# Two-layer hybrid block on one core: variances placed earlier, squares of the second half later, evenly dealt pieces, reordered first loads and last residuals

## The chip, the cores and the metric

The kernel runs on one core of one Trainium2 chip. The metric is the device time of one execution in microseconds. A core has TensorE (PE, matrix products into PSUM), VectorE (DVE), ScalarE (ACT), GpSimd (POOL) and SyncE (SP, whose queue issues most DMAs).

## The reference

All numbers are fp32; one sequence of 512 tokens, width 1024, two layers. What is computed:

```
for layer in range(2):
    a = rmsnorm(h, ln_mix_pre[layer]);  mem_n = rmsnorm(mem, ln_mem[layer])    # mem: 256 x 1024
    if layer == 0:
        u, v, q_mem = split(a @ w_in_a)                    # 768, 768, 256
        main = chunked_spatial_gating(u, v, ...)
    else:
        kvf = rmsnorm(h, ln_shared) @ w_shared_kv          # keys 768, values 768, 12 forget gates
        q, q_mem = split(a @ w_in_b)
        main = forgetting_attention(q, k, v, log_sigmoid(gates + b_forget))    # 12 heads of 64, causal
    mixed = concat(main, memory_attention(q_mem, mem_n, w_mem_kv[layer]))      # 4 memory heads
    h = h + rmsnorm(mixed @ w_out[layer], ln_mix_post[layer])
    f = rmsnorm(h, ln_ffn_pre[layer])
    f = (silu(f @ w_gate) * (f @ w_up)) @ w_down           # 1024 -> 2816 -> 1024
    h = h + rmsnorm(f, ln_ffn_post[layer])
```

The forgetting attention adds c_i - c_j to the logits, where c is the running sum of the log gates over the tokens. The last h is the output.

## The kernel before

**Products.** Each fp32 operand is split into a high part (a cast on ScalarE) and a low part (a subtraction on VectorE), and a product is three matmuls of such parts, lines 193 to 195: hi by hi, hi by lo, lo by hi. Weights come by DMA into tiles named raw; `split` makes whi and wlo of them (L241), `scaled_parts` (L245, L246) does the same with a gain. Most matmuls have 512 or 256 columns.

**Layout.** h holds the residual stream with the 1024 features as 8 blocks of 128 partitions and the 512 tokens along the row. The root mean square of a token is thus a sum over partitions: squares are added up on VectorE (acc, L279; for pairs of blocks sq, L320 and L322), multiplied by a column of 1/1024 on TensorE (st, L290), eps is added on VectorE (var, L292), GpSimd takes the power -1/2 (r, L262), TensorE spreads the result over the partitions (rb, L259), and VectorE copies it to rbc or rmem (L305) or uses it from PSUM. `Norm.finish` is the part up to r, `Norm.spread` the rest. Where tokens lie on partitions (the end of a mixer or an FFN, and value blocks) the scale is a column and is applied by ScalarE.

**Order.** The program is written as one stream of calls, and a list scheduler turns it into one list of instructions per engine. It takes them by the place in the program, `tc.high_priority()` moves what is inside it ahead, and `tc.issue_after(x)` (also through `behind`) holds an instruction until x stands. Engines run their lists in order and wait on semaphores.

**Start (layer A).** `layer_a` loads two blocks of query weights (raws, 128 x 1024 each) and the tokens. Per block k of the features TensorE multiplies both weight blocks with `ahi`, `alo`; behind the first products stand idle matmuls on zeros. Then come three value blocks in pieces (a piece is four blocks k for 128 tokens, 12 matmuls of 256 columns), among which the token norm, the memory's sums (`mem_sums`), its scaled inputs (`mem_inputs`, tiles mparts) and its key weights stand. `mem_project` makes the memory's keys and values.

**Boundary.** `boundary` joins the end of a mixer (or of an FFN) to the next projection. `tail(tb)` finishes 128 tokens and leaves them as y with tokens on partitions; `turn(half, pairs)` transposes y back (yt, L821), adds it to h (`residual`, L826), makes the scaled input of the next product and its squares (`nnorm.pair`). A `group` runs four weight blocks over the first half of the tokens; the turns of the second half hang in it after steps k = 3 and 5, and the norm of the first half after 6. Before the FFNs `combined` then adds and subtracts quarters of the inputs (lines 931 to 936), as a fast matrix product needs.

**Heads of layer B.** `attend` runs 4 memory heads and 12 forgetting heads one after the other, each in fixed steps (logits S, softmax N, transposes T, values V). At its F steps it takes pieces out of `between[n]`: for n = 0 to 11 those of the key and value projections (48 pieces: value block 0, key blocks 0 and 1, value block 1, key blocks 2 and 3 and so on), for n = 12 to 16 those of the output projection. `forget` makes the log gates (ScalarE and VectorE), `cumulate` their running sums (cs, 8 matmuls, L1251; then cc, four copies and differences, L1255 to L1258), and `head_parts` copies rows of cc and of the split queries and keys into qa, qc, ka, kc by DMAs of SP (L1281 to L1284).

**End.** `give(tb, ...)` transposes the FFN's result of 128 tokens back, adds it to h and stores it; for the last tokens this is four groups of two blocks, whose stores alternate between the queues of SP and ScalarE.

Of the kernel before, what the change touches and what calls it, by code (L numbers as in the profile page):

```python
# [40 lines left out]
def hybrid(ctx: ExitStack, tc: tile.TileContext, i: dict, out: bass.AP):  # L41
# [222 lines left out]
    class Norm:  # L264
# [16 lines left out]
        def finish(self, cols):  # L281

            c0, c1 = cols
            tbs = range(c0 // P, c1 // P)
            t0, t1 = c0 // P, c1 // P
            st = ps("tr", (P, 4), s="st")
            for tb in tbs:
                some = self.sums(tb, cols)
                for n, sq in enumerate(some):
                    PE.matmul(st[:, tb : tb + 1], sq, avg, start=n == 0, stop=n == len(some) - 1)  # L290
            v = small("var")
            V.tensor_scalar_add(v[:, t0:t1], st[:, t0:t1], RMS_EPS)  # L292
            rsqrt(self.r4[:, t0:t1], v[:, t0:t1], t1 - t0)

# [270 lines left out]
    def layer_a():  # L565
# [18 lines left out]
        tokens(0, 1)  # L584
        query_weights(1, 0, 1024)
        tokens(1, 2)
        tokens(2, 4)
        query_weights(0, 512, 1024)
        tokens(4, 6)
        tokens(6, 8)  # L590
# [30 lines left out]
        with tc.tile_pool(name="sgu", bufs=1) as lp:  # L621
# [8 lines left out]
            def pieces(n):  # L630
                for f in take(fill, n):
                    f()
# [9 lines left out]
            pieces(1)  # L642
            pre.spread(FULL, rbc)
            qf = [plain("q") for _ in range(2)]
# [3 lines left out]
            pieces(1)  # L648
            xs = mem_inputs(0, memt)
            wk = mem_key_weights(0)  # L650
            norm.finish((0, NMEM))
            pieces(3)
            norm.spread((0, NMEM), rmem)
# [105 lines left out]
    def tail_of(xs, load, ys, eps=None, last=False):  # L759
# [7 lines left out]
        def urgent(tb):  # L767
            return tc.high_priority() if tb == TB - 1 and not last else ExitStack()

# [87 lines left out]
    def boundary(phase, post, pre, nnorm, dst, block, evac, scaled=None):  # L857
# [8 lines left out]

        def turn(half, pairs):
            cols = HALVES[half]
            c0, c1 = cols
            for j in pairs:  # L870
# [7 lines left out]
                if scaled is not None:  # L878
# [4 lines left out]
                    xs[j, half] = pair_parts("xs", scaled[j, half])  # L883
                nnorm.pair(j, cols)

        def inputs(half):
# [3 lines left out]
            return [tuple(t[:, c0:c1] for t in xs[k]) for k in range(KT)]  # L890

        tail(0)
        phase_parts = tuple(last_parts)
        tail(1)
        with behind(phase_parts):
# [6 lines left out]
        outs = group(ws, inputs(0), h0, ["mm", "lg"] * 2, lag=3,  # L902
                     after={3: lambda: turn(1, range(2)), 5: lambda: turn(1, range(2, 4)),
                            6: lambda: nnorm.finish(h0)})
        nnorm.spread(h0, dst)
        evac(outs, h0)
        outs = group(ws[:2], inputs(1), h0, ["mm", "lg"])
        nnorm.finish(h1)
# [5 lines left out]

        return xs, close

# [125 lines left out]
    def feed_forward(layer, phase, xp, meanwhile=None):  # L1042
# [39 lines left out]

        scaled = {}
        a, close = boundary(phase, G_MIX_POST + layer, G_FFN_PRE + layer, nnorm, rb, first, evac_first, scaled)
        w = [down_weights(layer, 0, dh) for dh in range(2)]
        close()
        xs, last = combined(a, scaled, xp)
        last()
# [40 lines left out]
    def layer_b(phase, fp):  # L1129
# [16 lines left out]
        def evac_first(outs, cols):  # L1146
            for m, o in zip(first, outs):
                queries(m, o, cols)

        a, close = boundary(phase, G_FFN_POST, G_MIX_PRE + 1, bnorm, rbc,  # L1150
                            lambda n: prepared(i["w_b_q"][first[n]], (KT, P)), evac_first)
# [150 lines left out]
        more = queue(outs)  # L1302
        between = {n: take(fill, c) for n, c in enumerate((5, 5, 5, 5, 4, 4, 4, 4, 3, 3, 3, 3))}
        between[1].insert(4, forget)
        between[2].insert(3, cumulate)
        for n, c in zip(range(12, 17), (2, 3, 3, 4, 4)):
# [19 lines left out]
    with tc.tile_pool(name="ffn1", bufs=4) as xp:  # L1326
        tail, ys = feed_forward(1, phase, xp)

    def give(tb, order, queues=(nc.sync,)):

# [15 lines left out]
    idle(8, zero, end)  # L1346
    give(TB - 1, (range(4, 6), range(2), range(6, 8), range(2, 4)), (nc.sync, nc.scalar))

# [60 lines left out]
```

## Time and profile before

| | |
|---|---|
| median of 3 runs | 1121.24 us (1120.61 to 1121.42) |
| the profiled execution | 1121.42 us |
| its span, first to last instruction | 1119.7 us |
| granted TensorE clock, mean | 0.999 |
| TensorE, VectorE, ScalarE, GpSimd busy | 1107.3, 892.0, 660.3, 28.5 us |
| instructions | 19536 |
| DMA traffic | 118.12 MB |

Busy times are sums over instructions; matmuls overlap in TensorE's pipeline, so that a busy TensorE can still pause. In a row of the timeline stand the start in us, the duration in us, the engine, the line of the kernel, the operation, the tiles (written <- read), the shapes and the count; brackets give the idle time of the engine just before it and what ended that.

### The profile page before, as it was taken

What the parts mean: (1) busy time and instruction counts of PE and PEld (TensorE: products, weight loads), DVE (VectorE), ACT (ScalarE), POOL (GpSimd) and SP (SyncE); (2) the same over time, 40 slices, a digit from 0 to 9 for tenths busy, and PEclk for the clock granted to TensorE, in tenths of its full rate; (3) what the DMA queues carried; (4) which work ended last, traced back from release to release, by engine and by line L of the source; (5) the groups of instructions that cost most, each with busy time, mean ns of one, the idle gap of its engine ahead of it and who ended that gap; (6) DMA issues with size and microseconds to landing.
All of it is one profiled execution on the core that took longest, in us unless ns stands there. A gap on an engine that the chain in (4) does not pass through costs nothing.

```text
span 1119.7 us, 19536 instructions
## 1 busy us (share of the span) xinstructions
PE 1107.3 (99%) x7409; PEld 1002.7 (90%) x7409; DVE 892.0 (80%) x1721; ACT 660.3 (59%) x1388; POOL 28.5 (3%) x41
## 2 busy tenths in 40 slices
PE   8999999999999999999999999999999999999998
PEld 6998889999899899998988898889999899899996
DVE  7979448999598578796968889958998598588776
ACT  7775458755266255476757677768765266255453
POOL 0100001000000000001000000001000000000000
PEclk9999999999999999999999999999999999999999
DMA  7413231334224234244242655421235234233222
GB/s 265 151 49 109 77 97 58 100 108 151 76 89 140 74 99 127 76 135 148 63 128 59 153 128 137 135 76 57 65 106 152 74 101 133 70 109 118 76 76 76
DMA packets 63557, 118.12 MB, mean 105 GB/s; under 512 B 5164, under 2 KB 39992, under 8 KB 63464
## 3 DMA queue, kind: packets, MB, share of 16 engines
q1 hardware_dynamic: 62584, 116.05, 33.8%
q8 instruction: 58, 0.95, 0.4%
q0 software_dynamic: 192, 0.52, 0.2%
q10 hardware_dynamic: 688, 0.31, 0.1%
q14 instruction: 35, 0.29, 0.1%
HBM read 104.71 MB, written 2.10 MB: 95 GB/s over the span
## 4 chain that ended last, share of the span: by engine, by line
PE 86%; DVE 7%; ACT 3%; issue 2%; POOL 1%; DMA 1%; SPq 0%; POOLq 0%; DVEq 0%; ACTq 0%
PE y L193 9%; PE y L195 9%; PE y L194 9%; PE a L194 5%; PE a L193 5%; PE a L195 5%; PE ps L195 3%; PE ps L194 3%; PE ps L193 3%; PE e L193 3%; PE e L194 3%; PE x L194 3%; PE x L193 3%; PE x L195 3%; PE e L195 3%; DVE wlo L241 2%
## 5 line engine op out<-in xcount | busy, mean ns | idle before, releaser
L241 ACT CAST whi<-raw 128x512 fp32r<-128x512 f32 x460 | 276.2, 620 | 267.0 <-PE y L195 118.6
L241 DVE TENSOR_TENSOR wlo<-raw,whi 128x512 fp32r<-128x512 f32 x460 | 305.2, 685 | 108.8 <-ACT whi L241 106.6
L193 PE MATMUL y<-whi,fhi 128*128 128x512 f32 (+1 forms) x356 | 140.0, 394 | 0.0
L194 PE MATMUL y<-wlo,fhi 128*128 128x512 f32 (+1 forms) x356 | 139.4, 392 | 0.0
L195 PE MATMUL y<-whi,flo 128*128 128x512 f32 (+1 forms) x356 | 139.4, 392 | 0.0
L194 PE MATMUL a<-xslo,whi 128*128 128x256 f32 x320 | 90.0, 281 | 0.0
L194 PE MATMUL x<-xslo,whi 128*128 128x256 f32 x320 | 89.9, 281 | 0.0
L195 PE MATMUL x<-xshi,wlo 128*128 128x256 f32 x320 | 89.9, 281 | 0.0
L193 PE MATMUL x<-xshi,whi 128*128 128x256 f32 x320 | 89.8, 281 | 0.0
L193 PE MATMUL a<-xshi,whi 128*128 128x256 f32 x320 | 89.8, 281 | 0.0
L195 PE MATMUL a<-xshi,wlo 128*128 128x256 f32 x320 | 89.8, 281 | 0.0
L193 PEld LDWEIGHTS y<-whi,fhi 128*128 128x128 f32 x356 | 66.9, 188 | 15.7 <-ACT fhi L241 0.7
L195 PEld LDWEIGHTS y<-whi,flo 128*128 128x128 f32 x356 | 66.9, 188 | 15.5 <-DVE flo L241 0.2
L194 PEld LDWEIGHTS y<-wlo,fhi 128*128 128x128 f32 x356 | 67.0, 188 | 14.7 <-DVE wlo L241 0.2
L193 PE MATMUL ps<-xshi,whi 128*128 128x256 f32 (+1 forms) x224 | 67.5, 304 | 0.0
L195 PE MATMUL ps<-xshi,wlo 128*128 128x256 f32 (+1 forms) x224 | 67.1, 302 | 0.1
L194 PE MATMUL ps<-xslo,whi 128*128 128x256 f32 (+1 forms) x224 | 66.4, 299 | 0.0
L193 PEld LDWEIGHTS a<-xshi,whi 128*128 128x128 f32 x320 | 60.4, 189 | 0.4
L194 PEld LDWEIGHTS a<-xslo,whi 128*128 128x128 f32 x320 | 60.3, 188 | 0.3
L193 PEld LDWEIGHTS x<-xshi,whi 128*128 128x128 f32 x320 | 60.4, 189 | 0.0
L195 PEld LDWEIGHTS x<-xshi,wlo 128*128 128x128 f32 x320 | 60.3, 189 | 0.0
L194 PEld LDWEIGHTS x<-xslo,whi 128*128 128x128 f32 x320 | 60.3, 188 | 0.0
(283 smaller groups left out, 3091.1 us busy)
## 6 DMA issues: line engine op xcount, KB each, us to landing
raw<-in_w_gate SPq DMA_DIRECT2D x44, 512.0 KB, 3.6
raw<-in_w_up SPq DMA_DIRECT2D x44, 512.0 KB, 3.5
raw<-in_w_down SPq DMA_DIRECT2D x44, 512.0 KB, 4.0
raw<-in_w_out SPq DMA_DIRECT2D x16, 512.0 KB, 4.5
raw<-in_w_b_q SPq DMA_DIRECT2D x8, 512.0 KB, 3.5
raw<-in_w_a_v SPq DMA_DIRECT2D x6, 512.0 KB, 7.0
raw<-in_w_a_u SPq DMA_DIRECT2D x6, 512.0 KB
raw<-in_w_v SPq DMA_DIRECT2D x6, 512.0 KB, 3.7
```

The costliest lines, as they stand in the source:

```text
L193: PE.matmul(o, w[0], x[0], start=start, stop=False, skip_group_check=more)
L194: PE.matmul(o, w[0], x[1], start=False, stop=False, skip_group_check=more)
L195: return PE.matmul(o, w[1], x[0], start=False, stop=stop, skip_group_check=more)
L241: last_parts[:] = A.copy(hi, src), (eng or V).tensor_sub(lo, src, hi)
```

## The change

Six edits:

1. *Norm.finish*: eps and rsqrt are taken with high priority, and the rsqrt in pieces of two columns; the token norm of layer A is spread in two halves, one piece after its variance and another between the halves; the memory's variance stands ahead of its key weights, and two pieces instead of three ahead of its spread.
2. *First loads*: the second query block is loaded in two halves of 512, the second one behind the first token blocks.
3. *boundary*: the turns of the second half hang at steps 4 and 5 instead of 3 and 5, without their squares; the squares are made after the first half's results are given out. In the FFN `combined` is held behind the last of these turns.
4. *Heads*: four pieces for each n from 0 to 11 (before 5, 5, 5, 5, 4, 4, 4, 4, 3, 3, 3, 3); `forget` at the start of n = 2, `cumulate` at the start of n = 3 (before within 1 and 2).
5. *tail*: the high priority of the last block's tail also holds at the very end.
6. *give_last*: for the last 128 tokens two of the four groups use the other PSUM tag, are scaled by ScalarE and added by VectorE at once; three of the four stores go to SP, the last to ScalarE's queue.

```diff
@@ finish @@
-            V.tensor_scalar_add(v[:, t0:t1], st[:, t0:t1], RMS_EPS)
-            rsqrt(self.r4[:, t0:t1], v[:, t0:t1], t1 - t0)
+            with tc.high_priority():
+                V.tensor_scalar_add(v[:, t0:t1], st[:, t0:t1], RMS_EPS)
+                for t in range(t0, t1, 2):
+                    rsqrt(self.r4[:, t : t + 2], v[:, t : t + 2], 2)
@@ layer_a, first loads @@
-        query_weights(1, 0, 1024)
-        tokens(1, 2)
-        tokens(2, 4)
+        query_weights(1, 0, 512)
+        with tc.issue_after(last_load[0].ins):
+            tokens(1, 2)
+            tokens(2, 4)
         query_weights(0, 512, 1024)
+        query_weights(1, 512, 1024)
@@ layer_a, norms @@
             pieces(1)
-            pre.spread(FULL, rbc)
+            pre.spread(HALVES[0], rbc)
+            pieces(1)
+            pre.spread(HALVES[1], rbc)
...
             xs = mem_inputs(0, memt)
+            norm.finish((0, NMEM))
             wk = mem_key_weights(0)
-            norm.finish((0, NMEM))
-            pieces(3)
+            pieces(2)
             norm.spread((0, NMEM), rmem)
@@ tail_of @@
-            return tc.high_priority() if tb == TB - 1 and not last else ExitStack()
+            return tc.high_priority() if tb == TB - 1 else ExitStack()
@@ boundary @@
-        def turn(half, pairs):
+        def turn(half, pairs, sums=True):
...
-                nnorm.pair(j, cols)
+                if sums:
+                    nnorm.pair(j, cols)
...
-                     after={3: lambda: turn(1, range(2)), 5: lambda: turn(1, range(2, 4)),
+                     after={4: lambda: turn(1, range(2), False), 5: lambda: (turn(1, range(2, 4), False),
+                                                                                    turned_parts.extend(last_parts)),
                             6: lambda: nnorm.finish(h0)})
         nnorm.spread(h0, dst)
         evac(outs, h0)
+        for j in range(KT // 2):
+            nnorm.pair(j, h1)
@@ feed_forward @@
-        xs, last = combined(a, scaled, xp)
+        with behind(turned_parts):
+            xs, last = combined(a, scaled, xp)
@@ layer_b @@
-        between = {n: take(fill, c) for n, c in enumerate((5, 5, 5, 5, 4, 4, 4, 4, 3, 3, 3, 3))}
-        between[1].insert(4, forget)
-        between[2].insert(3, cumulate)
+        between = {n: take(fill, 4) for n in range(12)}
+        between[2].insert(0, forget)
+        between[3].insert(0, cumulate)
@@ the last tokens @@
+    def give_last(tb, queues):
+        c0, c1 = tb * P, (tb + 1) * P
+        at = slice(c0, c1)
+        for n, (k0, k1) in enumerate(((4, 6), (0, 2), (6, 8), (2, 4))):
+            tr = ps("tr" if k0 >= 4 else "mm", s="yt")
+            for x, k in enumerate(range(k0, k1)):
+                turned(ys, k, (tb,), tr[:, x * P : (x + 1) * P])
+            if k0 >= 4:
+                for x, k in enumerate(range(k0, k1)):
+                    residual(tr[:, x * P : (x + 1) * P], k, (c0, c1), G_FFN_POST + 1)
+            else:
+                t = temp("g", (P, 2, P))
+                for x, k in enumerate(range(k0, k1)):
+                    A.activation(t[:, x, :], tr[:, x * P : (x + 1) * P], AF.Copy, scale=gain(G_FFN_POST + 1, k))
+                V.tensor_add(h[:, k0:k1, at], h[:, k0:k1, at], t)
+            queues[k0 == 2].dma_start(out[:, k0:k1, at], h[:, k0:k1, at])
-    give(TB - 1, (range(4, 6), range(2), range(6, 8), range(2, 4)), (nc.sync, nc.scalar))
+    give_last(TB - 1, (nc.sync, nc.scalar))
```

What the edits move is decided by the scheduler. First VectorE at the first variance of layer A; acc_360 and acc_377 are the memory's running sum, mparts the memory's scaled inputs, wlo the low parts of the value weights, q_ the two query results. Before:

```order
L292 TENSOR_SCALAR var_323<-st_318 128x4
L279 TENSOR_TENSOR acc_360<-acc_360,sq_368 128x512
L246 SCALAR_TENSOR_TENSOR mparts_384<-mem_326,gains,mparts_384 128x256
L246 SCALAR_TENSOR_TENSOR mparts_387<-mem_326,gains,mparts_387 128x256
L305 COPY rbc<-rb_349 128x512
L246 SCALAR_TENSOR_TENSOR mparts_390<-mem_327,gains,mparts_390 128x256
L646 SCALAR_TENSOR_TENSOR q_355<-ps_181,rbc 128x512
L646 SCALAR_TENSOR_TENSOR q_356<-ps_182,rbc 128x512
```

And of the change, the same place:

```order
L293 TENSOR_SCALAR var_324<-st_319 128x4
L279 TENSOR_TENSOR acc_377<-acc_377,sq_385 128x512
L241 TENSOR_TENSOR wlo_391<-raw_388,whi_390 128x512
L307 COPY rbc<-rb_351 128x256
L307 COPY rbc<-rb_368 128x256
L241 TENSOR_TENSOR wlo_395<-raw_388,whi_394 128x512
L652 SCALAR_TENSOR_TENSOR q_372<-ps_182,rbc 128x512
L652 SCALAR_TENSOR_TENSOR q_373<-ps_183,rbc 128x512
L241 TENSOR_TENSOR wlo_401<-raw_398,whi_400 128x512
L293 TENSOR_SCALAR var_451<-st_446 128x2
```

A second subtraction stands behind the variance, the copy has become two, the mparts are gone from between, and the memory's variance (the last row) comes ahead of them.

Next VectorE at the boundary into the first FFN; var_2213 and var_2205 are the variance of the first half, sq_2120 and sq_2240 the squares of the second half, hs and xslo its scaled inputs, gr the first gate result. Before:

```order
L826 SCALAR_TENSOR_TENSOR h<-yt_2180,gains,h 128x256
L320 TENSOR_TENSOR sq_2120<-sq_2120,sq_2177 128x512
L241 TENSOR_TENSOR xslo_2174<-hs_2170,xshi_2173 128x512
L826 SCALAR_TENSOR_TENSOR h<-yt_2180,gains,h 128x256
L292 TENSOR_SCALAR var_2213<-st_2210 128x2
L931 TENSOR_TENSOR hs_1937<-hs_1937,hs_2113 128x512
L305 COPY rbc<-rb_2228 128x256
```

And of the change:

```order
L241 TENSOR_TENSOR xslo_2133<-hs_2129,xshi_2132 128x512
L293 TENSOR_SCALAR var_2205<-st_2202 128x2
L832 SCALAR_TENSOR_TENSOR h<-yt_2176,gains,h 128x256 x2
L241 TENSOR_TENSOR xslo_2147<-hs_2143,xshi_2146 128x512
L307 COPY rbc<-rb_2220 128x256
L241 TENSOR_TENSOR xslo_2173<-hs_2169,xshi_2172 128x512
L1063 TENSOR_TENSOR gr_2224<-ps_2058,rbc 128x256
L322 TENSOR_TENSOR sq_2240<-sq_2240,sq_2242 128x512
```

The variance now has two of the residual additions behind it, where the first of the combinations stood, and the squares come after the first gate result.

Last SP's queue at the first forgetting heads; qc_6901 and kc_6903 (of the change qc_6905 and kc_6907) belong to the first head, qc_6902 and kc_6904 (qc_6906 and kc_6908) to the second. Before:

```order
L1281 DMA qc_6901<-whi_7353 64x512
L1281 DMA qc_6902<-whi_7353 64x512
L1281 DMA kc_6903<-wlo_7356 64x512
L1281 DMA kc_6904<-wlo_7356 64x512
L1283 DMA qc_6901<-cc 2x512
L1284 DMA kc_6903<-cc 2x512
L1283 DMA qc_6902<-cc 2x512
L1284 DMA kc_6904<-cc 2x512
L1281 DMA qa_7383<-whi_7353 64x512
L1281 DMA qa_7383<-wlo_7354 64x512
L1281 DMA ka_7384<-whi_7355 64x512 x2
```

And of the change:

```order
L1293 DMA qc_6905<-whi_7304 64x512
L1293 DMA qc_6906<-whi_7304 64x512
L1293 DMA qa_7340<-whi_7304 64x512
L1293 DMA qa_7340<-wlo_7305 64x512
L1293 DMA ka_7341<-whi_7306 64x512 x2
L1293 DMA kc_6907<-wlo_7307 64x512
L1295 DMA qc_6905<-cc 2x512
L1296 DMA kc_6907<-cc 2x512
L1293 DMA kc_6908<-wlo_7307 64x512
L1295 DMA qc_6906<-cc 2x512
L1296 DMA kc_6908<-cc 2x512
```

The first head's copies now all stand ahead of the second head's, and the copies of the gates stand behind those of its qa and ka.

More of the change, by code (lines that the diff above doesn't have):

```diff
@@ L890, in inputs @@
             return [tuple(t[:, c0:c1] for t in xs[k]) for k in range(KT)]
+        turned_parts = []
         tail(0)
@@ L913, in close @@
             evac(outs, h1)
-        return xs, close
+        return xs, close, turned_parts
     def pair_parts(s, src, room=None):
@@ L1083, in feed_forward @@
         scaled = {}
-        a, close = boundary(phase, G_MIX_POST + layer, G_FFN_PRE + layer, nnorm, rb, first, evac_first, scaled)
+        a, close, turned_parts = boundary(phase, G_MIX_POST + layer, G_FFN_PRE + layer, nnorm, rb, first, evac_first, scaled)
         w = [down_weights(layer, 0, dh) for dh in range(2)]
         close()
-        xs, last = combined(a, scaled, xp)
+        with behind(turned_parts):
+            xs, last = combined(a, scaled, xp)
         last()
@@ L1148, in evac_first @@
                 queries(m, o, cols)
-        a, close = boundary(phase, G_FFN_POST, G_MIX_PRE + 1, bnorm, rbc,
+        a, close, _ = boundary(phase, G_FFN_POST, G_MIX_PRE + 1, bnorm, rbc,
                             lambda n: prepared(i["w_b_q"][first[n]], (KT, P)), evac_first)
```

## Prediction

> **What bounds the kernel now.** I read first the page's busy times and chain, then the waits of TensorE, then the timeline around each wait that the change touches.
>
> ```profile
> span 1119.7 us, 19536 instructions
> PE 1107.3 (99%) x7409; PEld 1002.7 (90%) x7409; DVE 892.0 (80%) x1721; ACT 660.3 (59%) x1388; POOL 28.5 (3%) x41
> PE 86%; DVE 7%; ACT 3%; issue 2%; POOL 1%; DMA 1%; SPq 0%; POOLq 0%; DVEq 0%; ACTq 0%
> ```
>
> TensorE is busy 1107.3 of 1119.7 us and makes 86% of the chain. The change takes no product away, so all that it can win is in the 12.4 us in which TensorE is not busy, the pauses inside "busy" and the tail. The waits of TensorE say where that time is:
>
> ```profile
> PE rb L259 <- POOL r L262: 2.5, 4, 1.7
> ...
> PE yt L821 <- ACT y L814: 1.0, 2, 0.5
> PE ps L193 <- ACT whi L241: 0.7, 1, 0.7
> PE e L193 <- ACT s L1003: 0.4, 1, 0.4
> PE yt L821 <- DVE y L809: 0.4, 1, 0.4
> PE yt L821 <- DVE h L826: 0.4, 2, 0.2
> ```
>
> The columns are the total in us, the number of waits and the longest one. The largest is the broadcast of an inverse root (rb) that waits for GpSimd. Every edit aims at a row of this kind, each below 2.6 us, so the whole is a matter of a few tenths of a per cent. A measurement of this kernel can tell about 0.2% from no change, which is 2.2 us. The sum is made against the profiled execution: 1121.42 us, of which 1119.7 are the span and 1.7 lie outside it; the median of the three runs is 1121.24.
>
> **First loads.** The second query block (wq1) is loaded as two halves, and its second half goes behind the first four token blocks.
>
> ```profile
> 3.17 0.43 SPq L572 DMA_DIRECT2D raw<-in_w_a_q  x1
> ...
> 7.50 1.14 ACT L241 CAST whi<-raw 128x512 fp32r<-128x512 f32 x2 [2.04 <-DMA raw<-in_w_a_q]
> 8.17 0.49 PE L193 MATMUL ps<-ahi,whi 128*128 128x512 f32 x1 [0.69 <-ACT whi L241]
> 8.54 2.19 ACT L245 ACTIVATE ahi<-h,gains 128x512 fp32r<-128x512 f32 x3
> 9.36 0.75 DVE L246 SCALAR_TENSOR_TENSOR alo<-h,gains,ahi 128x512 fp32r<-128x512 f32 x1
> 10.16 0.50 PE L194 MATMUL ps<-alo,whi 128*128 128x512 f32 x1
> ...
> 0.00:24.00 24.00, 21.54 (x98) 14.68 (x99) 17.79 (x33) 18.92 (x34) 1.32 (x7) 1.00 0.82 309
> ```
>
> ScalarE waits 2.04 us for the 512 KB of wq1, TensorE 0.69 us for ScalarE; the second token block is only split after that (8.54 and 9.36), and the steady run of products starts at 10.16. The last row says that the DMAs move 309 GB/s in this stage. With 256 KB less ahead of it, the first half of wq1 lands 256 KB / 309 GB/s = 0.85 us earlier, and the token block behind it too, so I take 0.85 us off everything up to the first variance. At most the 2.04 us that ScalarE waits can go; at least nothing, if the token block then lands no earlier, since SP issues one DMA more on the way, and an issue takes 0.43 us (first row).
>
> **The two variances in line.** The token variance is taken in two rsqrts of two columns, and the weights of the second value block are split ahead of it.
>
> ```profile
> 25.29 0.16 DVE L292 TENSOR_SCALAR var<-st 128x4 f32<-128x4 f32 x1 [1.57 <-PE st L290]
> 25.37 0.69 DVE L279 TENSOR_TENSOR acc<-acc,sq 128x512 f32<-128x512 f32 x1
> 25.53 1.41 POOL L262 TENSOR_TENSOR r<-var,mhalf 128x4 f32<-128x4 f32 x1 [22.60 <-DVE var L292]
> ...
> 26.99 0.65 PE L259 MATMUL rb<-ident,r 128*128 128x128 f32 x4 [0.47 <-POOL r L262]
> ...
> 34.14 0.28 PE L193 MATMUL ps<-mparts,whi 128*128 128x256 f32 x1
> ...
> 34.34 2.48 DVE L241 TENSOR_TENSOR wlo<-raw,whi 128x512 fp32r<-128x512 f32 x4
> 34.49 2.89 POOL L262 TENSOR_TENSOR r<-var,mhalf 128x2 f32<-128x2 f32 x1 [7.56 <-DVE var L292]
> ...
> 37.44 0.43 PE L259 MATMUL rb<-ident,r 128*128 128x128 f32 x2 [1.73 <-POOL r L262]
> ...
> 41.31 1.29 DVE L241 TENSOR_TENSOR wlo<-raw,whi 128x512 fp32r<-128x512 f32 x2
> ```
>
> The two POOL rows are the key. The same two-column rsqrt takes 2.89 us while VectorE runs four subtractions (34.34 to 36.82) and ends 0.56 us after the last of them (37.38); the four-column one beside a single addition (25.37 to 26.06) takes 1.41 and ends 0.88 after it. So GpSimd gets on only when the run of TENSOR_TENSORs is over. In the changed order two of them stand behind the variance (the addition and one wlo), and they end at 25.37 + 2 x 0.61 + 0.08 = 26.67. The first rsqrt ends 0.56 later, the second again about 0.56 later, at 27.8 instead of 26.94: the wait at the first broadcast grows by 0.9 us. The other broadcast gains: its variance now comes before the splitting of the memory inputs, so its root is there long before TensorE, and the 1.73 us go. But what is late next is the first weight of the memory keys. From the variance on, VectorE now has to do the two TENSOR_TENSORs, the waits for r and for the second sum, four more wlo, two q, the copies and all eight mparts before it: I add up 11.3 us from 25.29, that is 36.6 on the old clock, where TensorE comes at 34.14 + 0.9. A new wait of about 1.5 us stands there, less the two products that it may start without it. VectorE bounds the rest of the stage: the weights of the memory values (41.31, 16.0 us after the variance) come about 16.4 us after it. So this part is worth +0.35 us against its time before, between -1.7 (nothing new is late) and +1.6 (the first wait doubles and the new one is full).
>
> [...]
>
> **The boundaries between the mixer and the FFN, twice, and into layer B.** The turns of the second half come one step later, their squares after the first half is given out.
>
> ```profile
> 176.17 0.33 PE L821 MATMUL yt<-ident,y 128*128 128x128 f32 x1 [0.51 <-ACT y L814]
> ...
> 178.47 1.66 ACT L241 CAST whi<-raw 128x512 fp32r<-128x512 f32 x3
> ...
> 187.18 0.98 POOL L262 TENSOR_TENSOR r<-var,mhalf 128x2 f32<-128x2 f32 x1 [11.82 <-DVE var L292]
> 188.22 0.19 PEld L259 LDWEIGHTS rb<-ident,r 128*128 128x128 f32 x2 [0.38 <-POOL r L262]
> ```
>
> The wait of 0.51 us at the transposes goes, since their y is scaled a step earlier than they come. It is mostly given back: the products behind need the casts of 178.47, and ScalarE has as much to do before them as it had. At 188.22 TensorE waits 0.38 us for the root: the variance will be followed by two residual additions out of PSUM before the next TENSOR_TENSOR, so this goes. The second half's root stands, as now, before a run of TENSOR_TENSORs, and its reader may wait 0.1. I take -0.3 us for each of the two FFN boundaries. The same order at layer B's boundary has only small waits to remove, and squares of the first half that stay: -0.2. Ends for all three: -1.9, if the 0.51 of both is kept too, and +1.0, if the combined inputs, now behind the turns, come late.
>
> **Four pieces for each of twelve heads.** Sixteen heads run one after the other, and pieces of key and value projections fill TensorE between their steps.
>
> ```profile
> 583.12 0.28 PE L473 MATMUL mlg<-memk,q 128*128 128x256 f32 x1
> ...
> 622.96 0.39 PE L504 MATMUL lg<-kc,qc 68*128 68x512 f32 x1
> 660.91 0.39 PE L504 MATMUL lg<-kc,qc 68*128 68x512 f32 x1
> 694.34 0.40 PE L504 MATMUL lg<-kc,qc 68*128 68x512 f32 x1
> ...
> 583.12:622.96 39.84, 39.84 (x275) 36.23 (x273) 33.07 (x86) 27.41 (x66) 0.00 (x0) 1.00 0.34 88
> ```
>
> Between the first two lg rows lie four heads with four pieces: 37.95 us, 9.49 each. Between the last two lie four with three: 33.43 us, 8.36 each. So a piece costs 1.13 us there, although its products alone take 1.41 (12 products at the pitch of 0.118 us): the heads with three pieces have 0.28 us of gaps more. The change moves four pieces from the memory heads (583.12 to 622.96, five each) to those four. That adds 4 x 1.13 = 4.5 us and takes away 4 x 1.41 = 5.6, if the memory heads shrink by all of it: -1.1 us. VectorE is busy 33.07 of their 39.84 us, and 34.2 would be left, so it hides nearly nothing more: this is the thin place. Ends: -2.0 and +4.5 (the memory heads stay as long as they are).
>
> The cumulative gates come later too. They are needed by SP's copies into the first head's qc and kc:
>
> ```profile
> 608.57 1.17 PE cs L1251 x8
> ...
> 612.92 0.68 DVE L1258 TENSOR_TENSOR cc<-cc,cs 12x512 fp32r<-12x512 f32 x1
> ...
> 614.86 0.47 SPq L1284 DMA_DIRECT2D kc<-cc  x1
> ...
> kc<-wlo SPq DMA_DIRECT2D x4, 128.0 KB, 2.2
> ```
>
> Before, 13.2 us lie between the end of cs (609.74) and the first lg that reads them (622.96). Afterwards 24 wide products (0.235 each) and small ones stand there, about 7.7 us. The gates are ready 3.9 us after cs now (613.60), and the last copy is issued 1.7 later; 2.2 us to landing, as the last row has it for the copies of the keys, leave nothing to spare: 3.9 + 1.7 + 2.2 = 7.8. But half of those 1.7 us go to the second head's copies, which now stand behind. I count no wait, with 2 us as the other end, since two more subtractions and a cast now stand ahead of the gates on VectorE and ScalarE.
>
> **The tail.** The last token block's residuals go half through ScalarE.
>
> ```profile
> 1113.66 2.75 DVE L826 SCALAR_TENSOR_TENSOR h<-yt,gains,h 128x128 f32<-128x128 f32 x9
> ...
> 1115.24 1.58 ACTq L1339 DMA_DIRECT2D out<-h  x2
> ```
>
> Nine instructions take 2.75 us, 0.305 each, and the last DMA follows them. Four of them become two additions of 256 columns, about 0.4 each: 5 x 0.305 + 0.8 = 2.3, -0.4 us, as long as ScalarE's four scalings, beside it, are not late. Ends: -0.7 and +0.5.
>
> **Sum.** -0.85 + 0.35 - 0.6 - 0.2 - 1.1 - 0.4 = -2.8 us: 1121.42 - 2.8 = 1118.6.
>
> **The rivals.**
> - **VectorE gives it back.** In the first 57 us VectorE is the bound and the 0.85 us are eaten by its new order; at the boundaries the waits only move. That leaves -0.1 for the start, -0.2 for all boundaries, and the last two terms: 1119.6 at best, and 1120.2 where the heads win half. For it: the casts of 178.47; against it: the roots' waits are TensorE's own.
> - **The memory heads don't shrink** (the other side). The first lg waits for the copies of the gates, or VectorE, whose 33.07 us hold, for its turn. Each us not won there stays against 4.5 us added behind it. With the other terms at -1.7 it turns into a loss once the memory heads shorten by less than 2.8 us instead of 5.6; with nothing won there it is 1121.42 - 1.7 + 4.5 = 1124.2, and 1126.2 with the 2 us of the first lg on top.
> - **More stalls go than counted.** The four-piece heads lose their own gaps, both transposes' waits are kept: -2.0 for the heads, -1.2 for the boundaries, -0.9 for the start, -0.6 at the end: 1116.7.
> - **GpSimd gets in between two VectorE instructions.** If the first root is ready after the addition alone, 0.6 us earlier, and the second with it, the first broadcast waits no longer than now: 1118.0. [...]
> - **The change does not do what it says**: the variance stays behind the splitting. The order shows it moved, so this has no chance of its own.
>
> **How the numbers follow.** Forecast 0.36, VectorE gives it back 0.26, memory heads 0.18, more stalls 0.13, GpSimd in between 0.07. The time is the forecast's, 1118.6. Faster by over 0.2% means below 1119.0: more stalls, GpSimd and three quarters of the forecast, 0.47. Slower by that much, above 1123.5, is the upper half of the memory heads' times (1121.4 to 1126.2), 0.10. The rest, 0.43, is the same. The range leaves out some two thirds of the slower rival and little else: from 1116.6 (more stalls) to 1122.4.
>
> **What would show it.** Right: the second rb without a wait and a wait at the first ps<-mparts product instead; two POOL rows at the first variance that end about 2.5 us after it; rb near 188 without a wait; heads of about 9.4 us throughout, with the memory heads near 8.5; the first lg not waiting for kc. Wrong: a memory head as long as now; rb of the second half waiting over 0.5 us; a last DVE row later than 2.4 us after the scaled y.

## The result, and the profile after

| | before | after |
|---|---|---|
| median | 1121.12 us (1120.61 to 1122.37, 6 runs) | 1127.55 us (1125.83 to 1128.76, 6 runs) |
| ratio, 95% interval | | 1.0055 [1.0042, 1.0068] |
| the profiled execution, its span | 1121.42, 1119.7 us | 1128.76, 1127.0 us |

The changed kernel is 6.4 us slower; the forecast was 2.8 us faster. The page of the changed kernel, in the rows that answer to those shown of before (span; busy times; chain):

```profile
span 1127.0 us, 19529 instructions
PE 1110.0 (98%) x7409; PEld 1003.9 (89%) x7409; DVE 891.6 (79%) x1720; ACT 662.5 (59%) x1392; POOL 26.1 (2%) x42
PE 76%; DVE 11%; ACT 5%; DMA 3%; issue 3%; SPq 1%; POOL 0%; POOLq 0%; DVEq 0%; ACTq 0%
```

TensorE does the same 7409 products, but has 76% of the chain instead of 86%; VectorE, ScalarE and the DMAs have taken that over. TensorE's waits in the changed kernel (total in us, number, longest; the code has moved by some lines, so that L1020 is the L1009 of before, L475 the L473):

```profile
PE y L193 <- DVE s L1020: 3.0, 2, 2.4
PE mlg L475 <- ACT mp L442: 1.7, 2, 1.3
...
PE rb L259 <- POOL r L262: 0.2, 1, 0.2
```

The waits that the edits aimed at are gone: rb for r fell from 2.5 us to 0.2. Larger ones stand in other places, and the first two rows name engines that no edit was meant to load. To find the stage, I compared the start of the same product in both traces (after minus before, us):

| place in the trace of before | 58 | 199 | 269 | 281 | 558 | 721 | 774 | 808 | 872 | 1110 | end of span |
|---|---|---|---|---|---|---|---|---|---|---|---|
| after minus before | -0.75 | -1.09 | -0.62 | +3.55 | +3.20 | +6.29 | +5.85 | +6.85 | +7.60 | +7.31 | +7.3 |

Up to 199 us this trace goes as forecast: -0.75 at the start, -0.34 at the first boundary (whether the edits earned this is taken up below). Then 4.2 us are lost within 12 us of the first FFN, 3.1 in the heads, and 1.75 in the second FFN (774 to 872). The traced execution is the slowest of the six, 1.2 us above their median: of the 4.2 us, 2.4 are a wait, and 1.7 are a lower granted clock behind it (0.51) that only some executions show (last section). I take the places in turn.

**The first FFN.** The same stretch of before, rows of VectorE, of SP's queue and of ScalarE:

```profile
261.38 1.88 DVE L241 TENSOR_TENSOR wlo<-raw,whi 128x512 fp32r<-128x512 f32 x3
263.19 0.41 DVE L1009 TENSOR_TENSOR s<-a,s 128x256 f32<-128x256 f32 x1
...
263.30 3.14 SPq L169 DMA_DIRECT2D raw<-in_w_down  x2
...
269.95 0.62 ACT L241 CAST whi<-raw 128x512 fp32r<-128x512 f32 x1 [1.32 <-DMA raw<-in_w_down]
...
271.37 0.36 ACT L997 COPY s<-a 128x256 f32<-128x256 f32 x1
```

And of the changed kernel, with ScalarE and TensorE behind:

```profile
261.32 1.28 DVE L241 TENSOR_TENSOR wlo<-raw,whi 128x512 fp32r<-128x512 f32 x2
262.52 0.41 DVE L1020 TENSOR_TENSOR s<-a,s 128x256 f32<-128x256 f32 x1
264.65 1.88 DVE L241 TENSOR_TENSOR wlo<-raw,whi 128x512 fp32r<-128x512 f32 x3
265.39 0.94 SPq L169 DMA_DIRECT2D raw<-in_w_down  x2
269.46 1.14 ACT L241 CAST whi<-raw 128x512 fp32r<-128x512 f32 x2 [2.58 <-DMA raw<-in_w_down]
270.01 0.27 PE L195 MATMUL a<-xshi,wlo 128*128 128x256 f32 x1
272.44 1.14 ACT L241 CAST whi<-raw 128x512 fp32r<-128x512 f32 x2 [1.83 <-DMA raw<-in_w_down]
273.09 1.29 DVE L241 TENSOR_TENSOR wlo<-raw,whi 128x512 fp32r<-128x512 f32 x2 [1.68 <-ACT whi L241]
273.48 0.36 ACT L1008 COPY s<-a 128x256 f32<-128x256 f32 x1
274.30 0.42 DVE L1020 TENSOR_TENSOR s<-a,s 128x256 f32<-128x256 f32 x1
274.77 0.50 PE L193 MATMUL y<-whi,fhi 128*128 128x512 f32 x1 [2.39 <-DVE s L1020]
```

Read it downwards. Before, three low parts stood ahead of VectorE's sum of the last results (s<-a); now two do, and the third follows 2.1 us later, behind other work. That third one gives the buffer of a down weight free: SP issues the load at 265.39 instead of 263.30. ScalarE's casts wait for the load, and behind them, in the same list, stands the COPY that empties PSUM. It has been due since the last a product (270.01, ended at 270.28) and runs at 273.48. VectorE's next sum (274.30) needs the COPY, and in VectorE's own list it also stands behind two subtractions (273.09) that wait for the same casts. TensorE's next y product waits for the sum. No instruction of this chain was edited; only its place in the lists moved.

### The profile page after: what moved, and what is told of

It reads as the page before. It is cut to its first block, busy times and chain, and to the rows that moved or that the text cites. A ratio compares the mean times of both kernels' runs of the same rounds, so it can differ in the third digit from the quotient of the medians.

```text
span 1127.0 us, 19529 instructions
## 1 busy us (share of the span) xinstructions
PE 1110.0 (98%) x7409; PEld 1003.9 (89%) x7409; DVE 891.6 (79%) x1720; ACT 662.5 (59%) x1392; POOL 26.1 (2%) x42
## 4 chain that ended last, share of the span: by engine, by line
PE 76%; DVE 11%; ACT 5%; DMA 3%; issue 3%; SPq 1%; POOL 0%; POOLq 0%; DVEq 0%; ACTq 0%
PE y L193 9%; PE y L194 9%; PE y L195 9%; PE ps L195 4%; PE ps L193 4%; PE ps L194 4%; PE a L193 4%; PE a L195 4%; PE a L194 4%; DVE wlo L241 4%; PE x L193 3%; PE x L195 2%; PE x L194 2%; PE e L193 2%; PE e L195 2%
```

## The experiments

The kernel before was run again beside them in each of three sessions; its medians there were 1121.6, 1121.6 and 1121.7 us (24 to 27 runs each). First the change was taken apart, an edit or two at a time, with the rest as before; the core of each diff is repeated.

**Edits 1 and 2 alone.**

```diff
+            with tc.high_priority():
...
+                for t in range(t0, t1, 2):
...
-        query_weights(1, 0, 1024)
+        query_weights(1, 0, 512)
```

> Edits 1 and 2 alone (variances first in line, two-column roots, two halves of the second query block), all else as before. Parts theory (each edit carries its own gain or loss, and they add): the two profiles stand 0.75 us apart at 58 us (58.27 before, 57.52 after) and this stays to the end, so 1120.4, -0.5 to -1.2 us; the high priority of the variance also acts at the boundaries, worth -0.3 to +0.3 there. Rival, interaction theory (the 6.4 us come from edits that disturb one another, such as a shift of the whole program against the weight loads): a shift of -0.75 us alone would already unsettle the FFN, and this kernel would be slower by 1 us or more.

Measured: 1121.59 us (1120.08 to 1123.28, 11 runs), ratio 0.9999 [0.9991, 1.0008].

**Edit 3 alone.**

```diff
-                     after={3: lambda: turn(1, range(2)), 5: lambda: turn(1, range(2, 4)),
+                     after={4: lambda: turn(1, range(2), False), 5: lambda: (turn(1, range(2, 4), False),
...
+        for j in range(KT // 2):
+            nnorm.pair(j, h1)
...
+        with behind(turned_parts):
+            xs, last = combined(a, scaled, xp)
```

> Edit 3 alone (turns of the second half a step later, squares behind, the combinations held behind the turns). Parts theory: it carries what was lost in the two FFNs between the boundary and the end of their first group (about +4.3 us in the first, of which 2.4 is the wait of TensorE at 274.8 for an evacuation that stands behind weight casts on ScalarE, and about 1.8 the lower clock after it; +1.7 in the second), less 0.3 at each boundary: +4 to +6 us, 1125 to 1127. Interaction theory: within 1 us of before.

Measured: 1127.4 us (1126.35 to 1128.85, 5 runs), ratio 1.0051 [1.0037, 1.0065]: +5.8 us.

**Edit 4 alone.**

```diff
-        between = {n: take(fill, c) for n, c in enumerate((5, 5, 5, 5, 4, 4, 4, 4, 3, 3, 3, 3))}
-        between[1].insert(4, forget)
-        between[2].insert(3, cumulate)
+        between = {n: take(fill, 4) for n in range(12)}
+        between[2].insert(0, forget)
+        between[3].insert(0, cumulate)
```

> Edit 4 alone (four pieces for each of twelve heads, gates later). Parts theory: +2.5 to +3.5 us, as the two profiles move apart by 3.0 us between 561 and 711 us; waits of 1.4 and 0.6 us at the memory heads' logits and 1.3 at the first forgetting head. Interaction theory: -1 us, as the record has it, since the heads would come on undisturbed.

Measured: 1124.38 us (1123.32 to 1126.56, 8 runs), ratio 1.0025 [1.0014, 1.0035]: +2.8 us.

**Edits 5 and 6 alone.**

```diff
-            return tc.high_priority() if tb == TB - 1 and not last else ExitStack()
+            return tc.high_priority() if tb == TB - 1 else ExitStack()
...
-    give(TB - 1, (range(4, 6), range(2), range(6, 8), range(2, 4)), (nc.sync, nc.scalar))
+    give_last(TB - 1, (nc.sync, nc.scalar))
```

> Edits 5 and 6 alone (the last residuals through ScalarE). Both theories: the last row of VectorE ends 0.3 us earlier against the scaled y, the last store by the other queue order takes it back: -0.5 to +0.2 us.

Measured: 1121.28 us (1120.28 to 1122.19, 11 runs), ratio 0.9998 [0.9989, 1.0006].

So the loss is in edits 3 and 4. The parts sum to 0.0 + 5.8 + 2.8 - 0.3 = +8.3 against the +6.4 of the whole. The intervals of edits 3 and 4 and of the whole are over 1 us wide to each side, so that this difference may be noise. The traces, one of each, differ in two places by about 1.3 us together: edit 3 alone loses 0.74 us at layer B's boundary (near 550) and 2.4 between 774 and 872, the whole change 0.1 and 1.75.

Next edit 3 was taken apart. **The turns of the second half at steps 4 and 5 alone**, with their squares and nothing held:

```diff
-                     after={3: lambda: turn(1, range(2)), 5: lambda: turn(1, range(2, 4)),
+                     after={4: lambda: turn(1, range(2)), 5: lambda: turn(1, range(2, 4)),
```

> Of the boundary edit only the step: the second half's first turns hang at step 4 instead of 3, with their squares, nothing held. Late-turns theory (the whole second half of the boundary, its weights and the buffers behind them come a step later, about 1 us, and the FFN pays this where weights are the bound): most of the 5.8 us of the whole edit, +3 to +6 us, with waits at the first x<-xshi,whi and at the first group's y<-whi,fhi. Rival, order theory (the loss comes from holding the combinations behind the turns, which puts VectorE's weight splits in another order): +0 to +1 us.

Measured: 1130.82 us (1129.89 to 1131.51, 4 runs), ratio 1.0080 [1.0066, 1.0094]: +9.2 us, more than the whole edit. Its timeline at the first boundary shows a loss that edit 3 does not have:

```profile
188.39 0.15 DVE L292 TENSOR_SCALAR var<-st 128x2 f32<-128x2 f32 x1
188.46 0.68 DVE L932 TENSOR_TENSOR hs<-hs,hs 128x512 f32<-128x512 f32 x1
188.72 2.52 POOL L262 TENSOR_TENSOR r<-var,mhalf 128x2 f32<-128x2 f32 x1 [13.42 <-DVE var L292]
...
190.26 0.42 DVE L322 TENSOR_TENSOR sq<-sq 128x256 f32<-128x256 f32 x1
191.29 0.19 PEld L259 LDWEIGHTS rb<-ident,r 128*128 128x128 f32 x2 [2.09 <-POOL r L262]
```

The late squares and subtractions run without a pause from 188.46 to 190.68, and GpSimd's root takes 2.52 us and ends 0.56 behind them, as the row of 2.89 us did in the trace of before. The second boundary has the same wait of 2 us, and behind that one the granted clock falls too (to 0.50, last section). The y wait of the first FFN is there as well (2.1 us).

**The squares behind the first half's results, alone:**

```diff
-                nnorm.pair(j, cols)
+                if sums:
+                    nnorm.pair(j, cols)
...
+        for j in range(KT // 2):
+            nnorm.pair(j, h1)
```

> Of the boundary edit only the squares: turns at steps 3 and 5 as before, the second half's squares after the first half is given out. Late-turns theory: VectorE is freed early, so -0.5 to -1 us. Order theory: -0.5 to +1 us. If instead the squares are what delays the splits of the weights, +2 us or more.

Measured: 1121.33 us (1120.57 to 1122.25, 11 runs), ratio 0.9997 [0.9988, 1.0006].

**The combinations held behind the turns, alone:**

```diff
-        xs, last = combined(a, scaled, xp)
+        with behind(turned_parts):
+            xs, last = combined(a, scaled, xp)
```

> Of the boundary edit only that the combinations are held behind the last turns of the second half. Late-turns theory: -0.3 to +1 us. Order theory: +3 to +6 us, with the wait of over 2 us at the first group's y<-whi,fhi.

Measured: 1124.31 us (1123.62 to 1126.9, 11 runs), ratio 1.0026 [1.0017, 1.0035]: +2.7 us. Here the boundary has no new wait at all; the y product waits 2.37 us at 274.35, and again in the second FFN. So the wait at y does not need the late turns: holding the combinations back is enough to move the one subtraction behind the s<-a. The measured loss lies between the ranges of the two theories.

**Edit 3 with the splits of the last down weights, ScalarE's casts and VectorE's subtractions, held behind the COPY that empties PSUM**, in the first group of each FFN. This takes the blocking away and leaves the late load:

```diff
-            split(four[:, :, x, :], hi, lo)
+            with behind(hold):
+                split(four[:, :, x, :], hi, lo)
...
-                A.copy(s1[:, right], self.p)
+                copied[0] = A.copy(s1[:, right], self.p)
...
-                    w = down_weights(layer, k0 + 2 * kp, dh)
+                    w = down_weights(layer, k0 + 2 * kp, dh, hold=copied if gi == 0 and dh == 0 and kp == nk // 2 - 1 else ())
```

> The whole boundary edit, and the splits of the last down weights of the first group's first half held behind the evacuation (COPY s<-a) that TensorE waits for at 275 us; nothing else is changed. If the 2.4 us wait there, and the stretch of slower products behind it, come from casts on ScalarE (and subtractions on VectorE) that wait for late weights in front of that evacuation, both go and this is 2.5 to 4 us faster than the whole boundary edit (1123.5 to 1125). If the wait is a matter of the weights themselves, TensorE waits for whi at the same place instead and the time stays at 1126.5 to 1127.5.

Measured: 1124.09 us (1123.05 to 1124.33, 11 runs), ratio 1.0020 [1.0011, 1.0029]: 3.3 us less than edit 3 alone. Its timeline:

```profile
271.71 0.37 ACT L1003 COPY s<-a 128x256 f32<-128x256 f32 x1 [3.52 <-PE a L196]
271.98 1.15 ACT L242 CAST whi<-raw 128x512 fp32r<-128x512 f32 x2
272.21 0.40 PE L194 MATMUL y<-whi,fhi 128*128 128x512 f32 x1
```

The COPY now comes 0.04 us after the last a product has ended, ahead of the casts, and no y product waits, although the loads are as late as in edit 3. That shows the cause: splits that wait for a load, ahead of the emptying of PSUM. The run moved the casts and the subtractions together and does not divide the wait between the two lists. What is left, 2.5 us, lies at the boundaries: this trace stands at +0.75 us against that of before ahead of the y products of the first FFN, and at +0.77 behind them. Edit 3 alone shows the largest piece, before the combined weights' products in the first FFN:

```profile
212.75 1.66 ACT L241 CAST whi<-raw 128x512 fp32r<-128x512 f32 x3 [0.90 <-DVE raw L980]
213.42 0.19 PEld L193 LDWEIGHTS x<-xshi,whi 128*128 128x128 f32 x1 [0.77 <-ACT whi L241]
```

VectorE makes the combined weights (raw, L980) later, since the combined inputs now stand ahead of them; ScalarE waits for it, and TensorE for ScalarE. Between 199 and 218 us (in the times of before) edit 3 alone falls back by 1.0 us, and between 790 and 808 by 1.4.

**The late turns with the squares behind, nothing held:**

```diff
-                     after={3: lambda: turn(1, range(2)), 5: lambda: turn(1, range(2, 4)),
+                     after={4: lambda: turn(1, range(2), False), 5: lambda: turn(1, range(2, 4), False),
...
+        for j in range(KT // 2):
+            nnorm.pair(j, h1)
```

> The turns of the second half one step later and their squares behind the first half's results, the combinations not held. Theory that the late turns are what costs: the roots' waits of the late turns alone (2.04 and 1.99 us) go with the squares, the list of ScalarE at the last group of the first FFN is that of edit 3, so that y<-whi,fhi waits 2 us or more there again: +4.5 to +6 us, 1126 to 1127.5, as edit 3. Rival, that holding the combinations costs 2.7 us by itself wherever the turns are: +3, near 1124.5, and no long wait at the first FFN's y.

Measured: 1126.16 us (1125.91 to 1127.66, 5 runs), ratio 1.0042 [1.0028, 1.0056]: +4.4 us. Its waits of TensorE:

```profile
PE rb L259 <- POOL r L262: 3.1, 5, 1.7
PE y L193 <- DVE s L1012: 3.1, 2, 2.2
```

The y waits are all there, and the roots' waits, 3.1 us, are back near the 2.5 of before. So in edit 3 the late turns cost, and the squares save 4.8 us of that (9.2 - 4.4). The hold adds some 1.4 (5.8 - 4.4), five runs against five whose intervals overlap, so that no cost of it beside the late turns is shown. Alone it costs 2.7; that it adds less here would fit that both do the same harm at y.

Edit 4 was split as well. **The gates' place alone:**

```diff
-        between[1].insert(4, forget)
-        between[2].insert(3, cumulate)
+        between[2].insert(0, forget)
+        between[3].insert(0, cumulate)
```

> Only the place of the gates: forget at the start of head 2, cumulate at the start of head 3, five, four and three pieces as before. Theory that the number of pieces is what costs in edit 4: within 0.5 us of before, no exponent of a memory head waits over 1 us. Rival, that the place of the gates and their two table loads costs: +1.3 to +2.5 us, with waits of mlg for mp as in edit 4.

Measured: 1123.92 us (1122.84 to 1124.96, 11 runs), ratio 1.0021 [1.0012, 1.003]: +2.2 us. The memory heads, from the first mlg to the first lg<-kc,qc, as a row of windows (from:to, us, then TensorE and the other engines), and the wait in them:

```profile
582.91:624.68 41.77, 40.66 (x274) 36.32 (x273) 32.78 (x87) 27.68 (x67) 0.00 (x0) 1.00 0.34 89
...
605.76 0.39 PE L473 MATMUL mlg<-memk,q 128*128 128x256 f32 x1 [0.65 <-ACT mp L440]
```

**The number of pieces alone:**

```diff
-        between = {n: take(fill, c) for n, c in enumerate((5, 5, 5, 5, 4, 4, 4, 4, 3, 3, 3, 3))}
+        between = {n: take(fill, 4) for n in range(12)}
```

> Only the number of pieces: four for each of twelve heads, forget at the end of head 1 and cumulate within head 2 as before. Theory that the number of pieces costs: +2 to +3 us (1123.5 to 1124.5), the memory heads near 36 us instead of 39.8 and the eight next heads near 78 instead of 71.4. Rival, that the place of the gates costs: the memory heads near 34.5 us and the whole within 1 us of before.

Measured: 1122.71 us (1121.47 to 1123.29, 11 runs), ratio 1.0007 [0.9999, 1.0016]: +1.0 us. The memory heads, and the first logits of the first, the fifth and the ninth forgetting head:

```profile
582.72:618.21 35.49, 34.56 (x222) 29.82 (x221) 28.81 (x77) 25.01 (x62) 0.00 (x0) 1.00 0.20 48
...
618.21 0.40 PE L504 MATMUL lg<-kc,qc 68*128 68x512 f32 x1
656.42 0.39 PE L504 MATMUL lg<-kc,qc 68*128 68x512 f32 x1
695.50 0.40 PE L504 MATMUL lg<-kc,qc 68*128 68x512 f32 x1
```

My theory that the pieces make the loss fell: the gates' place alone loses 2.2 us, and the interval of the pieces' 1.0 just reaches no change. The three starts show why that is so little: the memory heads are 4.35 us shorter than before, and heads 5 to 8 are 5.65 longer.

**Everything but the late turns, the hold and edit 4**, that is edits 1, 2, 5 and 6 and the squares:

```diff
+            with tc.high_priority():
...
+        query_weights(1, 0, 512)
...
+                if sums:
+                    nnorm.pair(j, cols)
...
+    give_last(TB - 1, (nc.sync, nc.scalar))
```

> Edits 1, 2, 5 and 6 and, of edit 3, only the squares behind the first half's results; turns at steps 3 and 5, nothing held, heads as before. Theory that the late turns, the hold and the dealt pieces make all of the loss: 1120.5 to 1122, no difference from before that can be told. Rival, that the parts that measure nothing apart cost or win together: over 1122.5, or below 1119.5.

Measured: 1121.96 us (1119.85 to 1123.27, 11 runs), ratio 1.0002 [0.9993, 1.0011]. The parts that cost nothing alone cost nothing together, and win nothing that can be told; the interval leaves room for -0.8 to +1.2 us.

## Why the prediction was wrong, step by step

**First loads (-0.85).** Not shown to exist. The trace of the change stands at -0.75 at 58 us, but kernels whose start is that of before stand there at -0.42 (edit 3 alone), -0.49 (edits 5 and 6) and -0.79 (edit 4): the start moves that much from execution to execution. The trace of before, from which I worked, is the latest of the eleven with the old start, which stand at -0.3 in the mean. The three with the new one stand at -0.75, -0.80 and -0.99, so that about half a us may be real, and the agreement with the forecast is in part luck. Timed, edits 1 and 2 give no difference. Their one trace shows where a gain can go: it is 1.4 us ahead of before at 856 us and 0.4 behind at 900, since in the second FFN the chain of the first one holds up y:

```profile
857.91 1.14 ACT L241 CAST whi<-raw 128x512 fp32r<-128x512 f32 x2 [1.21 <-DMA raw<-in_w_down]
858.95 0.36 ACT L1003 COPY s<-a 128x256 f32<-128x256 f32 x1
860.25 0.50 PE L193 MATMUL y<-whi,fhi 128*128 128x512 f32 x1 [1.52 <-DVE s L1015]
```

In the trace of before the same casts also wait for the load there (0.42 us), and y is not held up.

**The variances (+0.35).** The place was right, one price was wrong. The first stage of the changed kernel:

```profile
25.03 1.76 POOL L262 TENSOR_TENSOR r<-var,mhalf 128x2 f32<-128x2 f32 x2 [22.09 <-DVE var L293]
26.16 0.19 PEld L259 LDWEIGHTS rb<-ident,r 128*128 128x128 f32 x2 [0.47 <-POOL r L262]
26.84 0.19 PEld L259 LDWEIGHTS rb<-ident,r 128*128 128x128 f32 x2 [0.48 <-POOL r L262]
...
35.51 0.39 PE L195 MATMUL ps<-mparts,wlo 128*128 128x256 f32 x1 [0.99 <-DVE wlo L241]
```

Both roots end at 26.79, 2.0 us after the variance (24.78), where I had 2.5. The first did not wait until VectorE's two TENSOR_TENSORs were over (26.15) and 0.56 us beyond, since TensorE loads it at 26.16; that is the rival in which GpSimd gets in between. The root of 2.52 us above, beside four TENSOR_TENSORs without a pause, ended only 0.56 us behind the last of them. Both rows stand; these runs do not say what decides. The wait of 1.73 at the memory's rb went, and the new one at the first mparts product came, 0.99 us.

**The boundaries (-0.3 each and -0.2).** This is the step that failed most: -0.8 forecast, +5.8 measured alone. What I argued at the turns and roots holds:

```profile
184.58 0.87 DVE L832 SCALAR_TENSOR_TENSOR h<-yt,gains,h 128x256 f32<-128x256 f32 x2
184.83 0.70 POOL L262 TENSOR_TENSOR r<-var,mhalf 128x2 f32<-128x2 f32 x1 [10.22 <-DVE var L293]
185.84 0.38 PE L259 MATMUL rb<-ident,r 128*128 128x128 f32 x2
```

The root beside two residual additions takes 0.70 us, rb does not wait, and the first boundary won 0.34 us, as forecast. But the late turns are not needed for this: the trace of edits 1 and 2 alone wins 0.33 there, that of the squares alone 0.30, that of edit 3 alone 0.17. I priced the edit where it stands and stopped there. "If the combined inputs come late" was my other end, at +1.0 for all three boundaries; I did not follow what the combinations push back: the combined weights (x, about 1 us twice), and, 75 us behind the boundary, a subtraction that frees a weight buffer. The trace of before had the warning: the cast at 269.95 that waited 1.32 us for its load, ahead of the same COPY (271.37).

**The heads (-1.1).** The rival "the memory heads don't shrink" was half right. Lengths in us, from the starts of the rows named above:

| kernel | memory heads | heads 1 to 4 | heads 5 to 8 | 9 to the start of 12 |
|---|---|---|---|---|
| before (pieces 5, 4, 3, 0) | 39.84 | 37.95 | 33.43 | 24.31 |
| pieces alone (4, 4, 4, 0) | 35.49 | 38.21 | 39.08 | 23.76 |
| gates alone | 41.77 | 37.98 | 33.44 | 24.33 |
| edit 4 alone | 36.21 | 38.86 | 39.11 | 23.82 |

Two sizes failed, and one step was left out. "A piece costs 1.13 us there": heads 5 to 8 grow by 5.65, 1.41 for each piece, the full price of its products. I had taken the difference between heads 1 to 4 and heads 5 to 8 for the price of a piece, but they differ in more than that. And "-5.6": the pieces alone shorten the memory heads by 4.35, with the gates' place by 3.63. The rows of the changed kernel:

```profile
604.83 1.28 ACT L1246 ACT_TABLE_LOAD   x1
606.38 1.28 ACT L442 ACT_TABLE_LOAD   x1
607.68 0.47 ACT L442 ACTIVATE mp<-mlg,nmx 128x256 f32<-128x256 f32 x1
...
608.30 0.38 PE L475 MATMUL mlg<-memk,q 128*128 128x256 f32 x1 [1.27 <-ACT mp L442]
```

The logarithm of the gates and the exponent of the softmax each stand behind a table load of 1.28 us. Before, no mlg waited beside the pair of loads (602.03 and 604.06); with forget at the start of the next head's pieces one does. That TensorE has too few products beside the loads there is my reading of these rows, and no run moved the loads by themselves; with the gates' place alone the waits of mlg (0.65 and 0.36 us) are about half of the 1.93 us by which the memory heads grow. I had counted the gates' copies into the first head, which do not wait, and not the tables. The first lg did not wait for kc, as forecast. The lengths that I had set as a sign did not come: the changed kernel's memory heads take 36.21 us, 9.05 each where I had 8.5, and heads 1 to 8 take 9.8 each where I had 9.4.

**The tail (-0.4).** Right in size, without effect. VectorE's last addition ends 2.95 us after the first scaled y (1120.43 to 1123.38), before 3.29 (1113.12 to 1116.41): -0.34. But from there the end of the span is as far as it was, 6.6 us after that y in both.

```profile
1122.96 0.42 DVE L1356 TENSOR_TENSOR h<-h,g 128x256 f32<-128x256 f32 x1
1123.41 0.40 ACTq L1357 DMA_DIRECT2D out<-h  x1
```

The last store is issued by 1123.81 and the span ends 3.2 us later; before it was 2.9. What the additions won was lost behind the store; why it takes longer there is open. Alone, edits 5 and 6 measured -0.3, within the interval of no change.

## What to carry to other kernels

Where a scheduler writes each engine's list, price an edit not only where it stands: follow what it pushes back on every engine until something waits, above all a copy out of PSUM that stands in one list with casts that wait for loads. Filler is not worth the same everywhere: before moving it away from a stage, ask which long instruction it may have been covering (here, by my reading, two table loads of 1.28 us). And a gain of under a microsecond at the start of a kernel can't be read from one trace when the start itself moves by as much.

## What the runs showed of the hardware

**TensorE's clock fell after a wait of about 2 us, but not always.** The changed kernel right behind its y wait of 2.39 us, and the kernel with the combinations held, behind one of 2.37 (window, us, busy times, granted clock, DMA share, GB/s):

```profile
276.30:279.70 3.40, 3.40 (x10) 2.66 (x9) 3.32 (x6) 1.13 (x3) 0.00 (x0) 0.51 0.25 96
```

```profile
276.50:280.00 3.50, 3.50 (x16) 2.81 (x16) 3.30 (x6) 1.14 (x2) 0.00 (x0) 1.00 0.09 34
```

In 3.4 us ten products run, where sixteen run in 3.5 at full clock, and 3.40 x (1 - 0.51) = 1.7 us go on top of the wait. The traces of edit 3 alone (wait 2.22, granted clock 0.56 from 276.40 to 279.80) and of the late turns with the squares behind (2.19, 0.51 from 276.30 to 279.70) show such a drop too. The late turns alone do not show it behind their y wait (2.09, then 1.00 from 276.50 to 280.00); behind the root of the first boundary (1.88) the products of 256 columns start 0.12 us apart from 191.69 to 192.51, as they do ahead of it. They show it behind the root of the second boundary, where TensorE has no product for 1.83 us:

```profile
784.30:787.40 3.10, 3.10 (x17) 3.10 (x17) 1.59 (x4) 0.00 (x0) 0.00 (x0) 0.50 0.21 28
```

The same code can have the drop or not. Of the six executions of the changed kernel three have a mean granted clock of 0.997 or 0.998 and take 1128.38 to 1128.76 us, and three have 0.999 or 1.000 and take 1125.83 to 1126.72. With the combinations held it is four of eleven, at 1125.39 to 1126.90 us against 1123.62 to 1124.41. With the splits held behind the COPY, where y does not wait, all eleven have 0.999 or 1.000. That the drop behind y makes these differences is inferred: where the clock fell can be seen in the traced executions alone.

In these four traces waits of 1.83 to 2.39 us stood ahead of a drop; a wait of 2.09 in one of them, and the wait of 2.37 with the combinations held, stood ahead of none. What decides, these runs do not show.

**A change of ScalarE's table took 1.28 us and nothing visible beyond**, in the changed kernel: the second load ends at 607.66, and the exponent starts at 607.68.
